# Streamed weight tiles that begin at 16 offsets, run forwards and backwards, with six raw buffers in place of seven

## The chip, the cores and the metric

One core of one Trainium2 chip runs the kernel. The metric is the device time of one execution in microseconds (us).

## The reference

One decoder layer for one sequence of 256 tokens with 4096 channels, all in float32. A conditioning vector gives shift, scale and gate; the normalised input is modulated, projected to six parts, half of the channels go through a mixture of dilated attention windows and half through causal pooling, and an output projection with a gated residual and a last normalisation follows.

```python
mod = c_act @ w_ada[l] + b_ada[l]                      # 4096 x 12288
shift, scale, gate = jnp.split(mod, 3, axis=-1)
h = rmsnorm(x, norm_gain[l])
h = h * (1.0 + scale[:, None, :]) + shift[:, None, :]
proj = jnp.einsum('bsd,dn->bsn', h, w_in[l])           # 4096 x 12288
q, k, v, g_attn, u_pool, g_pool = jnp.split(proj, ..., axis=-1)
y_attn = longnet_mixture(q, k, v).reshape(B, S, D_ATTN) * jax.nn.silu(g_attn)
y_pool = multiscale_pool(u_pool, w_pool[l], pool_scale[l]) * jax.nn.silu(g_pool)
y = jnp.concatenate([y_attn, y_pool], axis=-1) @ w_out[l]   # 4096 x 4096
x = x + gate[:, None, :] * y
return rmsnorm(x, final_gain)
```

## The kernel before

All weights are read once from HBM in float32, about 490 MB. A matrix product keeps float32 accuracy by three products of rounded operands: `w = wh + wl` and `h = hh + hl`, each part rounded to the type float32r, and `wh*hh + wh*hl + wl*hh` is summed in PSUM.

The unit of work is a *piece*: two blocks of 128 input channels by 512 output columns, one *raw* tile of 128 x 1024 float32 (512 KB). `split_piece` (L228) takes a raw tile from a ring of `RAWB` = 7, has SyncE load it (L231), ScalarE round it into `wh` (L237), and VectorE subtract for the remainder `wl` (L238). `wh` and `wl` have three buffers each, and begin on a multiple of 512 bytes (`LINE`). `products` (L241) then streams the piece through TensorE: 12 matmuls of 128 x 128 by 512 columns (L248), 8 with `wh` and 4 with `wl` as the moving operand, and `hh` or `hl` as the stationary one. The output projection uses the same function with `yh` and `yl` for `hh` and `hl`; those lie in the slots called `sa`. Of the last chunk of the output projection, the last six pieces (`HELD`) are split into such slots as well, and their second token tile goes through `prods_of_tile` (L614).

The input projection has 24 column chunks of 32 blocks; `visit` runs over them while units of two `h` blocks become ready. Raw tiles of the conditioning matrix `w_ada` run in the same ring: each is loaded by SyncE (L195, later L558) and multiplied into an accumulator, `aacc` or `gacc`, by two VectorE instructions (L161). `build_h` makes `hf`, `hh` and `hl` of a unit (L221 to L224). The gate is spread over the partitions by a float32 matmul on L565, whose moving operand is `gacc`.

A scheduler of the Tile layer sets the order on each engine; rates such as `GATE2` say how many `w_ada` tiles go with a piece. All loads are issued by SyncE in order. A raw load waits for the last reader of the tile that it overwrites. In the output projection each chunk also loads `x` (L638) and a slice of `final_gain` into the single buffer `fg` (L640), which the chunk before reads last on L672.

Of the kernel before, what the change touches and what calls it, by code (L numbers as in the profile page):

```python
# [8 lines left out]
F32R = mybir.dt.float32r  # L9
# [4 lines left out]
P = 128  # L14
# [4 lines left out]
CH = 512  # L19
# [22 lines left out]
PIECE = 2  # L42
HELD = 6
SPARE = 0
RAWB = 7
WHB = 3
WLB = 3
PSB = 2
PSMB = 4
LINE = 512  # L50
RAW = PIECE * CH
# [4 lines left out]
def tile_hybrid_block(  # L56
# [17 lines left out]
    nc = tc.nc  # L74
# [4 lines left out]
    strm = ctx.enter_context(tc.tile_pool(name="strm", bufs=2))  # L79

    def slot_a(shape, dtype=F32):
        return accp.tile(shape, dtype, name="sa", bufs=16, align_bytes=LINE)
# [7 lines left out]
    def misc():  # L90
        return ps_m.tile([P, CH], F32, name="psm")

    def raw_tile():
        return strm.tile([P, RAW], F32, name="raw", bufs=RAWB)

# [31 lines left out]
    pt = misc()  # L127
# [75 lines left out]
    def build_h(u, acc, pool, xT):  # L203
# [10 lines left out]
        for a in range(0, uk, 2):  # L214
# [10 lines left out]
            for i in range(2):  # L225
                hs[kk + i] = (hh[:, i], hl[:, i])

    def split_piece(src, n, spare=False):  # L228
        rt = raw_tile()
        v = rt.rearrange("p (k n) -> p k n", n=CH)  # L230
        nc.sync.dma_start(out=v[:, 0:n], in_=src)  # L231
        if spare:
            wh, wl = [slot_a([P, PIECE, CH], F32R) for _ in range(2)]
        else:
            wh = strm.tile([P, PIECE, CH], F32R, name="wh", bufs=WHB, align_bytes=LINE)
            wl = strm.tile([P, PIECE, CH], F32R, name="wl", bufs=WLB, align_bytes=LINE)
        nc.scalar.copy(out=wh[:, 0:n], in_=v[:, 0:n])  # L237
        nc.vector.tensor_tensor(out=wl[:, 0:n], in0=v[:, 0:n], in1=wh[:, 0:n].bitcast(F32), op=ALU.subtract)  # L238
        return wh, wl

    def products(pt, hv, wh, wl, first, last):  # L241
        n = len(hv)
        seq = [(t, i, p, wh) for i in range(n) for t in range(NT) for p in range(2)]
        seq += [(t, i, 0, wl) for t in range(NT) for i in range(n)]
        for e, (t, i, p, w) in enumerate(seq):
            started = first and not any(q[0] == t for q in seq[:e])
            ended = last and not any(q[0] == t for q in seq[e + 1:])
            nc.tensor.matmul(pt[t], lhsT=hv[i][p][:, t * P:(t + 1) * P], rhs=w[:, i], start=started, stop=ended)  # L248

    chains = []  # L250
    pending = []
# [24 lines left out]
    def visit(ch, ka, kb):  # L276
        pt = ps.tile([P, NT, CH], F32, name="mm")
        npc = -(-(kb - ka) // PIECE)
        szs = [(kb - ka) // npc + (1 if i < (kb - ka) % npc else 0) for i in range(npc)]
        k = ka  # L280
        for n in szs:
            wh, wl = split_piece(wi_v[:, k:k + n, ch * CH:(ch + 1) * CH], n)
            hv = [hs[k + i] for i in range(n)]
            products([pt[:, t] for t in range(NT)], hv, wh, wl, k == ka, k + n == kb)
            k += n
            tick(n)
        if ka == 0:
            accs[ch] = (slot_b if 8 <= ch < 16 else slot_a)([P, NT, CH])
            nc.scalar.copy(out=accs[ch], in_=pt)  # L289
        else:  # L290
            nc.vector.tensor_tensor(out=accs[ch], in0=pt, in1=accs[ch], op=ALU.add)  # L291
# [186 lines left out]
    def pool_mix(g):  # L478
# [31 lines left out]
        def lin():  # L510
            yh[4 + g] = slot_a([P, HG, S], F32R)
            yl[4 + g] = slot_a([P, HG, S], F32R)
            po = [misc(), misc()]
            wv = w_pool[0, g].rearrange("(k p) n -> p k n", p=P)
            w = [split_piece(wv[:, 2 * a:2 * a + 2], 2) for a in range(2)]
            for d in range(4):
                o = po[d // 2][:, (d % 2) * S:(d % 2 + 1) * S]
                ds = slice(d * P, (d + 1) * P)
                for c_ in range(4):
                    wh, wl = w[c_ // 2][0][:, c_ % 2, ds], w[c_ // 2][1][:, c_ % 2, ds]  # L520
                    ph, pl = k["ph"][:, c_], k["pl"][:, c_]
                    nc.tensor.matmul(o, lhsT=wh, rhs=ph, start=(c_ == 0), stop=False)  # L522
                    nc.tensor.matmul(o, lhsT=wh, rhs=pl, start=False, stop=False)  # L523
                    nc.tensor.matmul(o, lhsT=wl, rhs=ph, start=False, stop=(c_ == 3))  # L524
            for d in range(4):
                y = late.tile([P, S], F32, name="y", bufs=2)
                nc.vector.scalar_tensor_tensor(out=y, in0=po[d // 2][:, (d % 2) * S:(d % 2 + 1) * S],
                                               scalar=psc[:, g * 4 + d:g * 4 + d + 1],
                                               in1=k["sg"][:, d], op0=ALU.mult, op1=ALU.mult)
                nc.scalar.copy(out=yh[4 + g][:, d], in_=y)  # L530
                nc.vector.tensor_tensor(out=yl[4 + g][:, d], in0=y, in1=yh[4 + g][:, d].bitcast(F32), op=ALU.subtract)
                ydone[4 + g] += 1
# [51 lines left out]
    for c, ch in enumerate(order):  # L584
# [5 lines left out]
        elif 12 <= ch < 16:  # L590
            i = ch - 12
# [38 lines left out]
    def out_chunk(n):  # L630
# [12 lines left out]
        while k < KT:  # L643
            m = min(PIECE, KT - k)
            if k + 2 * PIECE >= KT > k + PIECE:
                need_gate(n)
            wh, wl = split_piece(wo_v[:, k:k + m, cs], m, n == 7 and KT - HELD * PIECE <= k < KT - SPARE * PIECE)
            while not all(ydone[kk // HG] == HG for kk in range(k, k + m)):
                tick(0)
            yv = [(yh[kk // 4][:, kk % 4], yl[kk // 4][:, kk % 4]) for kk in range(k, k + m)]  # L650
            if n == 7 and k + m > KT - HELD * PIECE:
                held.append((yv, wh, wl))
                prods_of_tile(pt, 0, held[-1:], k + m == KT)
            else:
                products(pt, yv, wh, wl, k == 0, k + m == KT)
            k += m
            tick(m)
# [79 lines left out]
```

## Time and profile before

| | |
|---|---|
| runs | 1567.26 and 1571.35 us, median 1569.3 us |
| the profiled execution's own time | 1567.34 us |
| its span, first to last instruction | 1565.4 us |
| busy: TensorE, VectorE, ScalarE | 97%, 90%, 45% |
| DMA moved | 491.11 MB, 314 GB/s on average |
| mean granted TensorE clock | 0.997 |

Times in the profile are microseconds from the start of the span, unless ns is written. PE is TensorE, PEld its weight loads, DVE is VectorE, ACT ScalarE, SP SyncE (SPq its queue, which issues the loads). A matmul's recorded duration overlaps the next one's, so its pace is read from one start to the next.

### The profile page before, as it was taken

How to read it: one execution, taken by the hardware profiler on the slowest of the kernel's cores; microseconds unless marked ns; L12 is line 12 of the kernel's file. 1: busy time of each engine (PE TensorE's matmuls, PEld its weight loads, DVE VectorE, ACT ScalarE, POOL GpSimd, SP SyncE). 2: the span in 40 equal slices, each digit the busy share in tenths (PEclk: the TensorE clock that was granted, in tenths of full speed). 3: DMA queues.
4: the chain of work that ended last, by engine and by line, in shares of the span. 5: the costliest groups of instructions: out<-in, count | busy, mean ns of one | idle time of the engine just before them, and what ended most of it. 6: DMA issues, size and time to landing. Idle time of an engine off the chain costs nothing.

```text
span 1565.4 us, 20360 instructions
## 1 busy us (share of the span) xinstructions
PE 1516.3 (97%) x7043; PEld 1257.5 (80%) x7043; DVE 1405.4 (90%) x1759; ACT 697.6 (45%) x820; POOL 0.7 (0%) x5
## 2 busy tenths in 40 slices
PE   2999999999999999999999999999999999999997
PEld 2877888888888888888888888888898888888775
DVE  5988999999999998899999998989988788898886
ACT  4655344443443434344344344556554443444433
POOL 0000000000000000000000000000000000000000
PEclk9999999999999999999999999999999999999999
DMA  9999999999999999899999998867778899998886
GB/s 331 363 335 362 321 331 321 324 308 336 327 310 327 312 330 313 294 326 326 354 340 331 330 333 307 290 226 242 231 250 273 287 357 347 318 339 324 320 305 250
DMA packets 324087, 491.11 MB, mean 314 GB/s; under 512 B 19320, under 2 KB 150664, under 8 KB 323984
## 3 DMA queue, kind: packets, MB, share of 16 engines
q1 hardware_dynamic: 323984, 489.82, 92.2%
q8 instruction: 55, 0.90, 0.2%
q14 instruction: 48, 0.39, 0.1%
HBM read 485.55 MB, written 4.19 MB: 313 GB/s over the span
## 4 chain that ended last, share of the span: by engine, by line
PE 91%; DVE 3%; DMA 3%; issue 1%; ACT 1%; SPq 0%; DVEq 0%; ACTq 0%
PE mm L248 83%; DVE aacc L161 1%; PE psm L614 1%; PE psm L248 1%; DMA raw<-in_w_ada_dram 1%; DMA raw<-in_w_in_dram 1%; PE psm L208 1%; DVE wl L238 1%; ACT wh L237 1%; PE psm L523 0%; PE psm L524 0%; PE psm L522 0%; DMA sb<-in_x_dram 0%; DMA raw<-in_w_out_dram 0%; PE psm L565 0%
## 5 line engine op out<-in xcount | busy, mean ns | idle before, releaser
L237 ACT CAST wh<-raw 128x1024 fp32r<-128x1024 f32 x514 | 538.5, 1050 | 700.0 <-PE mm L248 497.9
L238 DVE TENSOR_TENSOR wl<-raw,wh 128x1024 fp32r<-128x1024 f32 x514 | 624.5, 1218 | 45.1 <-ACT wh L237 41.9
L248 PE MATMUL mm<-wh,hh 128*128 128x512 f32 x1536 | 605.4, 394 | 4.8 <-ACT wh L237 3.8
L248 PE MATMUL mm<-wh,hl 128*128 128x512 f32 x1536 | 599.6, 390 | 0.0
L248 PE MATMUL mm<-wl,hh 128*128 128x512 f32 x1536 | 414.2, 391 | 0.6 <-DVE wl L238 0.6
L161 DVE SCALAR_TENSOR_TENSOR aacc<-raw,cact,aacc 128x512 f32<-128x512 f32 x496 | 371.0, 748 | 31.4 <-DMA raw<-in_w_ada_dram 23.8
L248 PEld LDWEIGHTS mm<-wh,hh 128*128 128x128 f32 x1536 | 288.8, 188 | 67.0 <-ACT wh L237 7.2
L248 PEld LDWEIGHTS mm<-wl,hh 128*128 128x128 f32 x1536 | 288.4, 188 | 61.1 <-DVE wl L238 1.4
L248 PEld LDWEIGHTS mm<-wh,hl 128*128 128x128 f32 x1536 | 288.9, 188 | 58.3 <-issue 0.2
L248 PE MATMUL mm<-wh,sa 128*128 128x512 f32 x896 | 224.0, 392 | 1.9 <-ACT wh L237 1.9
L248 PEld LDWEIGHTS mm<-wh,sa 128*128 128x128 f32 x896 | 167.7, 188 | 39.7 <-ACT wh L237 3.4
L161 DVE SCALAR_TENSOR_TENSOR gacc<-raw,cact,gacc 128x512 f32<-128x512 f32 x248 | 185.5, 748 | 13.5 <-DMA raw<-in_w_ada_dram 9.8
L248 PE MATMUL mm<-wl,sa 128*128 128x512 f32 x448 | 119.8, 389 | 0.0
L291 DVE TENSOR_TENSOR sa<-mm,sa 128x1024 f32<-128x1024 f32 x92 | 112.1, 1218 | 8.5 <-PE mm L248 8.4
L248 PEld LDWEIGHTS mm<-wl,sa 128*128 128x128 f32 x448 | 84.0, 188 | 17.5
L291 DVE TENSOR_TENSOR sb<-mm,sb 128x1024 f32<-128x1024 f32 x48 | 58.5, 1219 | 7.3 <-PE mm L248 7.3
L328 PE MATMUL psm<-diag_r,sb 128*128 128x128 f32 x128 | 16.9, 300 | 15.9 <-DVE diag_r L320 15.9
L221 ACT ACTIVATE hf<-xT,s 128x256 f32<-128x256 f32 x32 | 17.5, 595 | 27.9 <-DVE s L213 27.9
L328 PEld LDWEIGHTS psm<-diag_r,sb 128*128 128x128 f32 x128 | 16.6, 215 | 16.1 <-DVE diag_r L320 16.1
L289 ACT COPY sa<-mm 128x1024 f32<-128x1024 f32 x16 | 16.3, 1016 | 14.2 <-PE mm L248 14.1
L248 PE MATMUL psm<-wh,sa 128*128 128x512 f32 x80 | 20.1, 394 | 1.4 <-ACT wh L237 1.4
L248 PEld LDWEIGHTS psm<-wh,sa 128*128 128x128 f32 x80 | 14.8, 188 | 5.3 <-ACT wh L237 2.2
(113 smaller groups left out, 618.1 us busy)
## 6 DMA issues: line engine op xcount, KB each, us to landing
raw<-in_w_in_dram SPq DMA_DIRECT2D x384, 512.0 KB, 5.7
raw<-in_w_ada_dram SPq DMA_DIRECT2D x512, 256.0 KB, 5.3
raw<-in_w_ada_dram SPq DMA_DIRECT2D x128, 512.0 KB, 6.5
raw<-in_w_out_dram SPq DMA_DIRECT2D x128, 512.0 KB, 6.8
sb<-in_x_dram SPq DMA_DIRECT2D x16, 512.0 KB, 6.4
raw<-in_w_pool_dram SPq DMA_DIRECT2D x8, 512.0 KB, 4.7
out_dram<-sb SPq DMA_DIRECT2D x16, 256.0 KB, 2.6
fg<-in_final_gain_dram SPq DMA_DIRECT2D x8, 256.0 KB, 4.7
```

The lines of the kernel that those rows point to most:

```text
L161: nc.vector.scalar_tensor_tensor(out=acc, in0=r, scalar=cact[:, kt:kt + 1], in1=init if kt == 0 else acc, op0=ALU.mult, op1=ALU.add)
L208: nc.tensor.matmul(pc[:, j:j + 1], lhsT=acc[:, j * P:(j + 1) * P], rhs=ones, start=True, stop=True)
L221: nc.scalar.activation(out=hf[:, i], in_=xT[:, kk + i], func=AF.Identity, scale=s12[:, 1, a + i:a + i + 1], bias=s12[:, 0, a + i:a + i + 1])
L237: nc.scalar.copy(out=wh[:, 0:n], in_=v[:, 0:n])
L238: nc.vector.tensor_tensor(out=wl[:, 0:n], in0=v[:, 0:n], in1=wh[:, 0:n].bitcast(F32), op=ALU.subtract)
L248: nc.tensor.matmul(pt[t], lhsT=hv[i][p][:, t * P:(t + 1) * P], rhs=w[:, i], start=started, stop=ended)
L289: nc.scalar.copy(out=accs[ch], in_=pt)
L291: nc.vector.tensor_tensor(out=accs[ch], in0=pt, in1=accs[ch], op=ALU.add)
L328: nc.tensor.matmul(px[:, i * S + t * P:i * S + (t + 1) * P], lhsT=xs[q][:, t, (2 * a + i) * P:(2 * a + i + 1) * P], rhs=diag_r[:, t], star ...
L614: nc.tensor.matmul(pt[t], lhsT=h[:, t * P:(t + 1) * P], rhs=w, start=False, stop=last and e == len(seq) - 1)
```

## The change

Every tile of `wh` and `wl` grows by 128 elements (512 bytes per partition), and the piece within it begins at one of 16 offsets of 0 to 124 elements, which change after every second piece. Every second piece is marked in `back`; for these, `stream` gives the matmul its moving operand and its PSUM output with step -1, so that column 511 goes first and each result lands where it did. The ring of raw tiles has 6 tiles in place of 7. No instruction is added or taken away. In the built program 6072 matmuls pass through `stream`, 3036 of them with step -1, and 5676 begin off a multiple of 512 bytes; the weight pieces of the pooling map are used as stationary operands and begin at the offsets too, read forwards.

```diff
-RAWB = 7
+RAWB = 6
+STARTS = (0, 1, 4, 8, 16, 24, 32, 40, 48, 56, 64, 80, 96, 112, 120, 124)
...
+    count = [0]
+    back = {}
+
+    def stream(out, w, i):
+        if w.offset is not None and back.get((w.tensor.name, w.offset)):
+            return out[:, ::-1], w[:, i, ::-1]
+        return out, w[:, i]
+
     def split_piece(src, n, spare=False):
...
-            wh = strm.tile([P, PIECE, CH], F32R, name="wh", bufs=WHB, align_bytes=LINE)
-            wl = strm.tile([P, PIECE, CH], F32R, name="wl", bufs=WLB, align_bytes=LINE)
+            o = STARTS[count[0] // 2 % len(STARTS)]
+            wh, wl = [strm.tile([P, RAW + P], F32R, name=m, bufs=b, align_bytes=LINE)[:, o:o + RAW].rearrange(
+                "p (k n) -> p k n", n=CH) for m, b in (("wh", WHB), ("wl", WLB))]
+            back[wh.tensor.name, wh.offset] = back[wl.tensor.name, wl.offset] = count[0] % 2 == 1
+            count[0] += 1
...
-            nc.tensor.matmul(pt[t], lhsT=hv[i][p][:, t * P:(t + 1) * P], rhs=w[:, i], start=started, stop=ended)
+            o, m = stream(pt[t], w, i)
+            nc.tensor.matmul(o, lhsT=hv[i][p][:, t * P:(t + 1) * P], rhs=m, start=started, stop=ended)
```

The scheduler answers the smaller ring with a few other places. On ScalarE in the input projection, where a unit of `h` is built (`hf` is the modulated input, `hh` its rounding), the order before is:

```order
L237 CAST wh<-raw 128x1024 x23
L221 ACTIVATE hf<-xT,s_4390 128x256 x2
L237 CAST wh<-raw 128x1024
L223 CAST hh<-hf 128x512
L237 CAST wh<-raw 128x1024 x23
L221 ACTIVATE hf<-xT,s_4919 128x256 x2
L223 CAST hh<-hf 128x512
```

and in the changed kernel, at the same place:

```order
L249 CAST wh<-raw 128x1024 x24
L222 ACTIVATE hf<-xT,s_4390 128x256 x2
L224 CAST hh<-hf 128x512
L249 CAST wh<-raw 128x1024 x23
L222 ACTIVATE hf<-xT,s_4919 128x256 x2
L224 CAST hh<-hf 128x512
```

The rounding of the first unit's `hh` stands ahead of one weight's rounding and no longer behind it. On SyncE in the output projection, at the end of a chunk (`raw` tiles of `w_out` and `w_ada`, and `fg`, which waits for L672 of the chunk before), the order before is:

```order
L558 DMA raw_11815<-in_w_ada_dram 128x2x512 [waits DMAHW3_49,DVE_49]
L231 DMA raw_11819<-in_w_out_dram 128x2x512 [waits DMAHW4_49,DVE_49]
L558 DMA raw_11837<-in_w_ada_dram 128x2x512 [waits DMAHW5_49,DVE_49]
L231 DMA raw_11841<-in_w_out_dram 128x2x512 [waits DMAHW6_49,DVE_49]
L640 DMA fg_11733<-in_final_gain_dram 128x512 [waits DVE_49]
L558 DMA raw_11859<-in_w_ada_dram 128x2x512 [waits DMAHW7_49,DMAHW0_49,Activation_49]
```

and in the changed kernel:

```order
L571 DMA raw_11815<-in_w_ada_dram 128x2x512 [waits DMAHW4_49,DVE_49]
L240 DMA raw_11819<-in_w_out_dram 128x2x512 [waits DMAHW5_49,DVE_49]
L571 DMA raw_11837<-in_w_ada_dram 128x2x512 [waits DMAHW6_49,DVE_49]
L653 DMA fg_11733<-in_final_gain_dram 128x512 [waits DVE_49]
L240 DMA raw_11841<-in_w_out_dram 128x2x512 [waits DMAHW0_49,Activation_49]
L571 DMA raw_11859<-in_w_ada_dram 128x2x512 [waits DMAHW7_49,DMAHW1_49,DVE_49]
```

The load of `fg` stands one raw load (raw_11841) earlier.

## Rows read from the trace of the kernel before

**Rows 1.** The page: busy time by engine, and the chain that ended last.

```profile
PE 1516.3 (97%) x7043; PEld 1257.5 (80%) x7043; DVE 1405.4 (90%) x1759; ACT 697.6 (45%) x820; POOL 0.7 (0%) x5
...
PE 91%; DVE 3%; DMA 3%; issue 1%; ACT 1%; SPq 0%; DVEq 0%; ACTq 0%
PE mm L248 83%; DVE aacc L161 1%; PE psm L614 1%; PE psm L248 1%; DMA raw<-in_w_ada_dram 1%; DMA raw<-in_w_in_dram 1%; PE psm L208 1%; DVE wl L238 1%; ACT wh L237 1%; PE psm L523 0%; PE psm L524 0%; PE psm L522 0%; DMA sb<-in_x_dram 0%; DMA raw<-in_w_out_dram 0%; PE psm L565 0%
```

**Rows 2.** Windows by stage: stretch, length, busy by engine, then clock, DMA share, GB/s.

```profile
60.00:300.00 240.00, 235.53 (x1037) 192.20 (x1036) 222.84 (x260) 114.43 (x118) 0.00 (x0) 0.99 0.99 334
300.00:900.00 600.00, 599.04 (x2682) 497.21 (x2681) 564.59 (x647) 241.35 (x244) 0.00 (x0) 1.00 0.97 325
900.00:1250.00 350.00, 349.41 (x1821) 294.14 (x1821) 312.65 (x491) 180.20 (x245) 0.53 (x1) 1.00 0.82 271
1250.00:1500.00 250.00, 248.06 (x1085) 203.15 (x1084) 219.20 (x241) 102.65 (x114) 0.00 (x0) 1.00 0.93 335
```

**Rows 3.** Timeline of TensorE over one piece: start, duration, what [idle before].

```profile
700.46 0.39 PE L248 MATMUL mm<-wh,hh 128*128 128x512 f32 x1
...
702.28 1.07 PE L248 MATMUL mm<-wl,hh 128*128 128x512 f32 x4
703.18 0.39 PE L248 MATMUL mm<-wh,hh 128*128 128x512 f32 x1
```

**Rows 4.** The same after a wait of TensorE near 80 us.

```profile
79.58 0.50 PE L248 MATMUL mm<-wh,hh 128*128 128x512 f32 x1 [2.05 <-ACT wh L237]
79.92 0.39 PE L248 MATMUL mm<-wh,hl 128*128 128x512 f32 x1
...
80.62 0.48 PE L248 MATMUL mm<-wh,hh 128*128 128x512 f32 x1
...
81.32 0.63 PE L248 MATMUL mm<-wh,hh 128*128 128x512 f32 x1
81.75 0.63 PE L248 MATMUL mm<-wh,hl 128*128 128x512 f32 x1
82.17 1.91 PE L248 MATMUL mm<-wl,hh 128*128 128x512 f32 x4
```

**Rows 5.** The same around the gate's broadcast at 1361 us.

```profile
1361.06 1.02 PE L565 MATMUL psm<-gacc,ones_m 128*128 128x512 f32 x2
1361.52 1.72 PE L248 MATMUL mm<-wh,sa 128*128 128x512 f32 x5
```

**Rows 6.** Waits of SyncE's queue: us in total, times, longest.

```profile
SPq L231 <- DVE wl L238: 324.2, 280, 5.4
...
SPq L640 <- DVE sb L672: 42.1, 7, 9.5
```

**Rows 7.** Waits of the engines, same columns.

```profile
ACT wh L237 <- PE mm L248: 497.9, 314, 4.3
ACT wh L237 <- DMA raw<-in_w_out_dram: 82.1, 49, 5.7
ACT wh L237 <- DMA raw<-in_w_in_dram: 81.3, 46, 3.9
...
PE mm L248 <- ACT wh L237: 5.8, 5, 2.0
```

**Rows 8.** The page's groups: count, busy us, mean ns, idle before and its releaser.

```profile
L237 ACT CAST wh<-raw 128x1024 fp32r<-128x1024 f32 x514 | 538.5, 1050 | 700.0 <-PE mm L248 497.9
L238 DVE TENSOR_TENSOR wl<-raw,wh 128x1024 fp32r<-128x1024 f32 x514 | 624.5, 1218 | 45.1 <-ACT wh L237 41.9
```

**Rows 9.** Loads of 300:900, 1250:1500 and 1020:1110 us: median us to landing.

```profile
raw<-in_w_in_dram SPq DMA_DIRECT2D x217, 512.0 KB, 5.6
...
raw<-in_w_out_dram SPq DMA_DIRECT2D x90, 512.0 KB, 7.0
...
DMA packets 11128, 21.53 MB, mean 239 GB/s; under 512 B 653, under 2 KB 653, under 8 KB 11122
...
raw<-in_w_in_dram SPq DMA_DIRECT2D x21, 512.0 KB, 4.7
```

**Rows 10.** Timeline of SyncE's queue at a chunk end.

```profile
1415.09 0.37 SPq L558 DMA_DIRECT2D raw<-in_w_ada_dram  x1
1423.23 0.35 SPq L640 DMA_DIRECT2D fg<-in_final_gain_dram  x1
```

**Rows 11.** Timeline at the next chunk end.

```profile
1472.94 1.04 ACT L237 CAST wh<-raw 128x1024 fp32r<-128x1024 f32 x1 [5.71 <-DVE gacc L161]
...
1474.03 2.11 PE L248 MATMUL mm<-wh,sa 128*128 128x512 f32 x8 [1.94 <-ACT wh L237]
```

## The prediction

> **What bounds the kernel now.** I read the busy shares and the chain first, then windows by stage, then single matmuls, then the rows of the ring of raw buffers. TensorE is busy 97% of the span, and 91% of the chain that ended last is its own work, 83% on the line of the streamed products; DMA holds 3% of the chain and VectorE 3% [rows 1]. So the price of one streamed matmul sets the time. From 700.46 to 703.18 us the twelve matmuls of one piece follow each other: 2.72 us, 226.7 ns each, while the clock is granted in full (1.00 in all middle windows, [rows 2, 3]). There are 512 streamed pieces (24 chunks of the input projection and 8 of the output projection, 16 each), 6144 matmuls: 6144 x 226.7 ns = 1393 us of the 1565.4. The rest is the start, attention and pooling on the same engine, waits and the end.
>
> DMA is close behind: its engines are 97 to 99% busy in the projections until 900 us, 82% in the next stage, 93% in the output projection [rows 2]. What hides it is the ring of raw tiles. SyncE nearly always finds the ring full and waits for a last reader, 280 times for the remainder on L238 alone [rows 6], while ScalarE waits 314 times for TensorE to give back a rounded tile and only 95 times for a weight to land [rows 7]; TensorE itself waits for a rounded tile in the products only 5 times, 5.8 us [rows 7].
>
> The profiled execution took 1567.3 us, its span and 1.9 us around it; the median of the runs is 2.0 us above it. Sums are made against 1567.3 and carried over to the median.
>
> **Part 1: the starts.** No instruction is added. In the built program 6072 of the 6144 streamed matmuls go through the new helper (72 of the last chunk read held tiles as before), and 5676 of them now begin off a 512-byte line, most of them by a multiple of 32 bytes. What that costs TensorE no row shows, since every streamed operand begins on a line. Three bounds. The nearest row is the gate's broadcast on L565, whose moving operand lies 288 bytes past a line (by the built program's addresses): its two records take 0.46 us, 230 ns for 512 columns, though in full fp32 [rows 5]. The dearest rows of aligned products at the full clock are those just after a wait: from 79.92 to 80.62 us three matmuls take 0.70 us, 233 ns each [rows 4]. So a price is 0 to 6.5 ns per matmul: 0 to 5676 x 6.5 = 37 us. Below nothing: the pace holds about 13 ns that don't scale with the clock. Between 81.32 and 82.17 us, right after a wait of 2.05 us, two matmuls take 0.85 us, 425 ns for the 512 columns [rows 4]; so the clock was at the lower of its two levels (1.2 and 2.4 GHz), and half of it is 213 ns, 13.5 less than 226.7. Were they a quarrel over where the two operands lie, up to 5676 x 13.5 = 77 us could go. I take 0: the pace is the same for the wh and the wl products, for both halves of a tile and beside any VectorE or ScalarE work in the stretch shown [rows 3], so no sign of a quarrel over addresses is in the trace. ScalarE's and VectorE's writes to the new starts are taken at nothing too: their 1050 and 1218 ns [rows 8] read a raw tile that lies 352 bytes past a line already, ScalarE is idle 700 us, and a slower write hides as long as the two rounded tiles ahead do.
>
> The Trainium skill's page "TensorE: Matmul & The Clock Gate" (Wait — 56ns, not 53.3ns?) gives 512 columns / 2.4 GHz + 2.5 ns, 215.7 ns, for such a stream; the rows show 226.7, so the measurement decides, and by the page alone 11 ns of each matmul would be there to win (about 62 us).
>
> **Part 2: back to front.** 3036 matmuls read the rounded tile and write PSUM with step -1. No row has a negative step on any engine. Nothing if the operand is fetched and written in the same groups either way. At the other end one column every second clock: that is the price at the clock's lower level, 0.43 us from 81.32 to 81.75 in place of 0.227 [rows 4], so 3036 x 0.2 = 607 us. I choose 0, as the same words are touched in the same lines, but keep the other end as a rival.
>
> **Part 3: six raw tiles.** A tile is 512 KB. In 300 to 900 us it comes every 524,288 B / 325 GB/s = 1.61 us, so with seven a tile lives 11.3 us: 5.6 to land [rows 9], 1.05 + 1.22 in its two readers [rows 8], 3.4 to spare. With six it is 9.7 us, 1.8 to spare: nothing lost. In the output projection (335 GB/s, 1.57 us) seven give 11.0: 7.0 to land, 2.3 read, 1.7 spare; six give 9.4 and 0.1 spare. That still carries the rate, since a landing shortens when fewer are under way (4.7 us at 239 GB/s [rows 9]), but there is no reserve. It is needed at the chunk ends, where the load of final_gain waits on SyncE for L672 with all later raw loads behind it: no issue between 1415.09 and 1423.23 us, and 42.1 us in 7 waits in all [rows 6, 10]. Mostly the ring covers that; at 1474.03 us it does not, and TensorE waits 1.94 us [rows 11]. One tile less is 1.57 us less cover: 0 to 7 x 1.57 = 11 us. I take 1.6 for the end that fails already and 0.7 for the other six: 6 us. Among the five early waits of TensorE (5.8 us, [rows 7]) I charge two with one tile: 3 us; there DMA is at its limit (99%) and the number of tiles matters less. A longer wait can cost clock as well: after the one of 2.05 us at 79.58, six matmuls ran at the lower level, some 1.2 us [rows 4]; two or three such are in the range.
>
> **Part 4: what moves.** The order shows hh's rounding ahead of a weight's cast and not behind it, on an engine with 700 us idle: 0. The load of final_gain stands one raw load earlier, which is the same lost tile.
>
> Sum: 0 + 0 + 6 + 3 = +9 us: 1576 for the profiled one, **1578 us** at the median. With the ring's ends 0 and +22 (11 at the chunk ends, 8 for all five early waits, 3 of clock) this case runs from 1566 to 1593.
>
> **Rivals.** (a) *A start off the line costs a little.* Every product off a line takes 230 to 233 ns: 19 to 37 us and the ring's 9, 1597 to 1615. For it: the two rows above. Against: one is fp32, the other aligned. It passes 2% from 4 ns per matmul (5676 x 4 = 23 us beside the 9). (b) *Back to front at half pace*, slower far over 2%: 1578 + 607 = 2185. The place is TensorE's stream of every second piece; it passes 2% from 7 ns per reversed matmul (3036 x 7 = 21 us beside the 9). For it: no row of a reversed stream exists, and the start of the stream is the only thing that the change does to TensorE's inner loop. The Trainium skill's page "PSUM — Partial Sum Buffer" (Specifications) speaks for it: it says that any output that is not contiguous slows matmuls; whether a step of -1 counts, no run here shows. (c) *The fixed 13.5 ns shrink.* 77 us less on TensorE, but DMA is busy 99, 97, 82 and 93% of the four windows [rows 2], which lets through 2 us of 240, 18 of 600, all of some 20 in 350, and 17 of 250, together 57: about 1521. Against: the pace knows no other value in the undisturbed stretches.
> That the change doesn't do what it says is excluded: the built program holds the starts and the steps.
>
> **Chances.** Forecast 0.61, (a) 0.19, (b) 0.15, (c) 0.05. The range goes from 1564, the forecast without any cost of the ring and a little scatter, to 1630, (a) at its dear end with the ring at its own (1569 + 37 + 22 = 1628); (b) and (c), 0.20, are left out. About 2%, 31 us, is what a measurement can tell from no change. Faster is (c), 0.05. Slower is (b) and most of (a): 0.30. Same is the forecast and the rest of (a): 0.65.
>
> **What would show it.** Right: the twelve matmuls of a piece in 2.72 us at every offset and in both directions; waits of TensorE for ScalarE's rounding around the chunk ends, some 1 to 3 us each; landings in the output projection near 6 us; fewer waits of ScalarE for TensorE and more for DMA. Wrong: two paces that alternate piece by piece (direction) or a cycle of 32 pieces (offset); or DMA's share falling below 0.9 in 300 to 900 us with TensorE waiting there, which would mean that the spare 1.8 us was not there.

## The result and the profile after

The changed kernel takes 1607.8 us (median; 1605.1 to 1610.6), before 1569.3 us: a ratio of 1.0247, 95% interval 1.0206 to 1.0288. It is slower by 38.5 us, beyond the 2% that counts as no change.

The page of the changed kernel, in the lines that answer to [rows 1]:

```profile
PE 1550.7 (97%) x7043; PEld 1257.4 (78%) x7043; DVE 1410.7 (88%) x1759; ACT 696.9 (43%) x820; POOL 0.7 (0%) x5
...
PE 89%; DMA 4%; DVE 3%; issue 2%; ACT 1%; SPq 1%; DVEq 0%; ACTq 0%
```

TensorE is as full as before, so the span of 1603.3 us (37.9 more) is not made of waits. The windows by stage, columns as in [rows 2]:

```profile
60.00:300.00 240.00, 234.87 (x1016) 187.03 (x1015) 219.66 (x255) 113.29 (x116) 0.00 (x0) 1.00 0.98 328
300.00:900.00 600.00, 598.06 (x2601) 483.00 (x2600) 552.05 (x627) 234.75 (x238) 0.00 (x0) 1.00 0.95 314
900.00:1250.00 350.00, 349.36 (x1804) 290.45 (x1803) 310.14 (x493) 175.74 (x238) 0.53 (x1) 1.00 0.82 270
1250.00:1500.00 250.00, 248.87 (x1062) 199.13 (x1061) 210.79 (x230) 98.31 (x110) 0.00 (x0) 1.00 0.92 323
```

Between 300 and 900 us 2601 matmuls fit where 2682 did, at the same full clock; DMA serves 314 GB/s where it served 325, and its engines are less busy, not more. The timeline of TensorE, as in [rows 3], shows where each matmul got dearer. The program's order tells which piece is which: at 327.19 us a piece at offset 0 forwards, at 329.94 one at offset 0 back to front, at 332.74 one at offset 1 forwards, at 335.59 the same back to front; at 364.44 one at offset 32 back to front.

```profile
327.19 0.39 PE L261 MATMUL mm<-wh,hh 128*128 128x512 f32 x1
...
329.03 1.07 PE L261 MATMUL mm<-wl,hh 128*128 128x512 f32 x4
329.94 0.40 PE L261 MATMUL mm<-wh,hh 128*128 128x512 f32 x1
...
331.81 1.10 PE L261 MATMUL mm<-wl,hh 128*128 128x512 f32 x4
332.74 0.40 PE L261 MATMUL mm<-wh,hh 128*128 128x512 f32 x1
...
335.59 0.40 PE L261 MATMUL mm<-wh,hh 128*128 128x512 f32 x1
...
364.44 0.40 PE L261 MATMUL mm<-wh,hh 128*128 128x512 f32 x1
...
367.32 0.39 PE L261 MATMUL mm<-wh,hh 128*128 128x512 f32 x1
```

From piece to piece: 2.75 us, 2.80, 2.85, and 2.88 us for the last; before, the piece of [rows 3] took 2.72. Over all undisturbed starts of the trace (from one start to the next under 250 ns) a streamed matmul takes 227.0 ns before and 233.2 after: 6144 x 6.2 = 38 us, as much as the span has grown. By direction it is 232.3 ns forwards and 234.1 back to front. Waits of the engines, as in [rows 7], tell that the ring has become tighter without TensorE noticing much:

```profile
ACT wh L249 <- PE mm L261: 462.9, 277, 7.6
ACT wh L249 <- DMA raw<-in_w_in_dram: 128.2, 76, 4.6
ACT wh L249 <- DMA raw<-in_w_out_dram: 114.0, 64, 5.9
```

ScalarE waits for a landing 140 times where it waited 95 times. ScalarE's rounding and VectorE's remainder cost what they cost, 1048 and 1220 ns (1050 and 1218 in [rows 8]), so writing at the new starts is free for them. The waits of SyncE's queue, as in [rows 6]:

```profile
SPq L240 <- DVE wl L250: 332.2, 237, 6.6
...
SPq L653 <- DVE sb L685: 18.9, 7, 4.2
```

The waits for `fg` at the chunk ends fell from 42.1 us to 18.9. That is no gain: the raw load ahead of `fg` now waits in its place. SyncE's queue at the chunk end that answers to [rows 10]:

```profile
1446.59 0.37 SPq L571 DMA_DIRECT2D raw<-in_w_ada_dram  x1
1452.68 0.37 SPq L240 DMA_DIRECT2D raw<-in_w_out_dram  x1
```

The load of `fg` follows at 1457.22 us. Over the seven chunk ends, the gap in the queue before `fg` and the one before the load ahead of it come to 51.8 us together in the kernel before and to 46.8 here.

### The profile page after: what moved, and what is told of

It is laid out like the page before. It is cut to its first block, busy times and chain, and to the rows that moved or that the text cites. A ratio compares the mean times of both kernels' runs of the same rounds, so it can differ in the third digit from the quotient of the medians.

```text
span 1603.3 us, 20336 instructions
## 1 busy us (share of the span) xinstructions
PE 1550.7 (97%) x7043; PEld 1257.4 (78%) x7043; DVE 1410.7 (88%) x1759; ACT 696.9 (43%) x820; POOL 0.7 (0%) x5
## 4 chain that ended last, share of the span: by engine, by line
PE 89%; DMA 4%; DVE 3%; issue 2%; ACT 1%; SPq 1%; DVEq 0%; ACTq 0%
PE mm L261 81%; DMA raw<-in_w_ada_dram 2%; DVE aacc L162 2%; DVE wl L250 1%; PE psm L627 1%; PE psm L261 1%; DMA raw<-in_w_out_dram 1%; DMA raw<-in_w_in_dram 1%; PE psm L209 1%; ACT wh L249 1%; DMA sb<-in_x_dram 0%; PE psm L537 0%; PE psm L535 0%; PE psm L536 0%; PE psm L424 0%
## 5 line engine op out<-in xcount | busy, mean ns | idle before, releaser
L249 ACT CAST wh<-raw 128x1024 fp32r<-128x1024 f32 x514 | 537.5, 1048 | 739.4 <-PE mm L261 462.9
L250 DVE TENSOR_TENSOR wl<-raw,wh 128x1024 fp32r<-128x1024 f32 x514 | 624.8, 1220 | 48.5 <-ACT wh L249 43.2
L261 PE MATMUL mm<-wh,hh 128*128 128x512 f32 x1536 | 614.0, 400 | 6.5 <-ACT wh L249 4.8
L261 PE MATMUL mm<-wh,hl 128*128 128x512 f32 x1536 | 609.1, 397 | 0.0
L261 PE MATMUL mm<-wl,hh 128*128 128x512 f32 x1536 | 423.5, 397 | 0.6 <-DVE wl L250 0.6
L261 PE MATMUL mm<-wh,sa 128*128 128x512 f32 x896 | 229.7, 399 | 3.1 <-ACT wh L249 3.1
L678 DVE TENSOR_TENSOR yo<-mm,gt 128x1024 f32<-128x1024 f32 x7 | 8.6, 1224 | 13.2 <-PE mm L261 13.2
```

What stands on the lines that cost most here:

```text
L261: nc.tensor.matmul(o, lhsT=hv[i][p][:, t * P:(t + 1) * P], rhs=m, start=started, stop=ended)
L678: nc.vector.tensor_tensor(out=y[:, tp], in0=src, in1=gt.unsqueeze(1).to_broadcast(w), op=ALU.mult)
```

## The experiments

All have six raw tiles and the padded rounded tiles of the changed kernel. The theory was that each streamed matmul got dearer by the place and direction of its operand; the rivals were the ring of six, and that only the *change* from one piece to the next costs. The pace is the mean from one start to the next over the undisturbed starts. The first four ran on one chip with the kernel before (1568.2 us there).

**e1_ring6: the ring alone.**

```diff
-STARTS = (0, 1, 4, 8, 16, 24, 32, 40, 48, 56, 64, 80, 96, 112, 120, 124)
+STARTS = (0,)
...
-            back[wh.tensor.name, wh.offset] = back[wl.tensor.name, wl.offset] = count[0] % 2 == 1
+            back[wh.tensor.name, wh.offset] = back[wl.tensor.name, wl.offset] = False
```

> The changed kernel with all tiles begun at offset 0 and read forwards: what is left of the change is the ring of six raw tiles (and the padding of the rounded tiles). Address theory (each streamed matmul costs more off a line or back to front, and that is all of the loss): a piece in 2.72 us, ratio 1.000 to 1.003. Rival, the ring as the prediction priced it: +9 us, ratio 1.006. Rival, the ring as the main cause: ratio 1.02.

Measured: 1579.4 us, ratio 1.0068 (1.0051 to 1.0085), by that ratio +10.7 us. The pace is 227.1 ns. So dearer matmuls alone would not be the whole story: the ring by itself costs about what the prediction charged for it, but not where. Waits of the engines and of SyncE's queue, and a part of TensorE's timeline, all of this run:

```profile
ACT wh L249 <- DMA raw<-in_w_in_dram: 197.6, 116, 4.7
ACT wh L249 <- DMA raw<-in_w_out_dram: 116.2, 63, 7.5
...
PE mm L261 <- ACT wh L249: 9.7, 8, 2.0
```

```profile
SPq L653 <- DVE sb L685: 18.9, 7, 4.2
```

```profile
594.67 0.77 PE L261 MATMUL mm<-wh,hh 128*128 128x512 f32 x1 [1.67 <-DVE sa L304]
...
627.26 0.96 PE L261 MATMUL mm<-wl,hh 128*128 128x512 f32 x3 [1.42 <-DVE wl L250]
...
651.52 0.47 PE L261 MATMUL mm<-wh,hh 128*128 128x512 f32 x1 [0.83 <-DVE sb L304]
...
675.72 0.47 PE L261 MATMUL mm<-wh,hh 128*128 128x512 f32 x1 [0.80 <-ACT wh L249]
...
1484.86 1.48 PE L261 MATMUL mm<-wh,sa 128*128 128x512 f32 x3 [2.02 <-ACT wh L249]
```

Counted from streamed matmul 2000 to 3000 (516 to 756 us), the run loses 7.3 us more than before, and 3.4 us more from 5500 to 6000 near the end; each of the other stretches of 500 differs by under 1 us. The larger part lies in the input projection, where the prediction had found 1.8 us to spare per tile and charged only the early waits. There, from 516 to 756 us, ScalarE waits 54 times for a `w_in` tile to land, 99.3 us in all, where before it waited 15 times, 29.3 us. VectorE, for which TensorE waits at 594.67, had itself waited 3.06 us for a `w_ada` tile. Some of the loss is clock: after the waits at 594.67 and 1484.86 five and eight matmuls run at 0.43 us each, the lower of its two levels (granted 0.50 from 595.2 to 597.4 us and 0.54 from 1484.8 to 1488.3), together some 3 us.

**e2_offsets: the 16 offsets, all forwards** (`back` set to False as in e1, `STARTS` left).

> The 16 offsets alone, every piece read forwards, six raw tiles. Address theory: in the trace of the changed kernel forward pieces go at 232.2 ns per matmul over all offsets, so 6144 x (232.2 - 227.0) = +32 us, about 1601. If the step -1 is what costs, and the offsets only look dear because every piece follows a reversed one: 1570 to 1575.

Measured: 1604.8 us, ratio 1.0236 (1.0215 to 1.0256); the pace is 232.2 ns. The offsets alone cost 5.1 ns per matmul, and 25 us beside e1.

**e3_alternate: every second piece back to front, all at offset 0** (`STARTS = (0,)`).

> Every second piece back to front, all at offset 0, six raw tiles. Address theory: back to front at offset 0 goes at 233.6 ns, forward pieces between them at 228.7, so 6144 x (231.1 - 227.0) = +25 us, about 1594. If the offsets are what costs: 1570 to 1575.

Measured: 1595.5 us, ratio 1.0172 (1.0153 to 1.0191); pace 233.6 ns back to front and 228.4 forwards.

**e4_all_back: every piece back to front, at offset 0** (`STARTS = (0,)`, `back` set to True).

> Every piece back to front, all at offset 0, six raw tiles. If the step itself costs: 233.6 ns per matmul, +40 us, about 1609, more than when every second piece is reversed. Rival, only the change from one piece to the next costs, as after a wait: 227 ns again, 1570.

Measured: 1610.8 us, ratio 1.0275 (1.0257 to 1.0292); 233.4 ns for every matmul. The direction itself costs 6.3 ns. So the rival that only the change of direction costs falls; only some 1.3 ns on the forward pieces of e3 come from it.

The others ran once each, with the kernel before at 1565.1 to 1570.7 us beside them. They are read against e1, and above all by their pace, a mean over more than 5700 starts.

**e9_read_back and e10_write_back: which side of the reversal costs.** Both from e4, with the helper's return cut in two:

```diff
-            return out[:, ::-1], w[:, i, ::-1]
+            return out, w[:, i, ::-1]        # e9
+            return out[:, ::-1], w[:, i]     # e10
```

> Every piece is read back to front at offset 0, but its PSUM output is written forwards, so each 512-column chunk comes out mirrored and the layer's output is changed by that; the work is the same. If the read of the moving operand is what costs 6.3 ns: 233.3 ns per matmul, about 1610. If the write to PSUM costs: 227 ns, about 1579.

> Every piece is read forwards at offset 0, but written to PSUM back to front, so each 512-column chunk comes out mirrored; the work is the same. If the PSUM write with step -1 costs: 233.3 ns per matmul, about 1610. If the read costs: 227 ns, about 1579.

Measured: e9 1611.0 us and 233.4 ns, e10 1580.8 us and 227.1 ns. One piece of TensorE's timeline in e9 and then in e10:

```profile
700.29 0.40 PE L261 MATMUL mm<-wh,hh 128*128 128x512 f32 x1
...
702.16 1.10 PE L261 MATMUL mm<-wl,hh 128*128 128x512 f32 x4
703.09 0.40 PE L261 MATMUL mm<-wh,hh 128*128 128x512 f32 x1
```

```profile
700.91 0.39 PE L261 MATMUL mm<-wh,hh 128*128 128x512 f32 x1
...
702.73 1.07 PE L261 MATMUL mm<-wl,hh 128*128 128x512 f32 x4
703.63 0.39 PE L261 MATMUL mm<-wh,hh 128*128 128x512 f32 x1
```

2.80 us against 2.72 for the piece: the read from SBUF with step -1 is the whole price, and the write to PSUM with step -1 is free.

**e5_start64, e6_start32, e7_start1: one offset throughout, forwards** (`STARTS = (64,)`, `(32,)`, `(1,)`).

> Every piece begins 64 elements (256 bytes) past a 512-byte line, forwards, six raw tiles. In the traces with 16 offsets this one reads like offset 0. If the cost goes by the address modulo 256 bytes: 227 ns per matmul, time as with the ring alone, about 1579. If a whole 512-byte line counts: 230 ns or more, 1595 and up.

> Every piece begins 32 elements (128 bytes) past a line, forwards, six raw tiles; the offset never changes. If the address itself costs: 233 ns per matmul as in the runs with changing offsets, about 1605. Rival, only a change of address from piece to piece costs: 227 ns, about 1579.

> Every piece begins 1 element (4 bytes) past a line, forwards, six raw tiles; stationary tiles on the line. Address theory: 236.8 ns per matmul as with changing offsets, 60 us over the ring alone, about 1639. If the change from piece to piece were part of that price: less, down to 233 ns, about 1616.

Measured: 1582.5 us at 227.1 ns; 1608.5 us at 232.5 ns; 1632.5 us at 237.8 ns. The address costs also when it never changes, and 256 bytes further on costs nothing. The time of e7 is 6 us under the one expected although its pace is above it: the starts that are 250 ns or more apart cost 24.2 us above the pace in e7 and 33.3 in e1, so at the slower pace the ring gives most of its own cost back.

**e8_both32 and e11_stat32: whose address it is.** The stationary tiles of the input projection are moved as well, with `STARTS = (32,)` in e8 and `(0,)` in e11; both give up one buffer of the attention scratch (`sm`, not shown):

```diff
-                htile[kk // HB] = [pool.tile([P, HB, S], F32R, name=n, align_bytes=LINE) for n in ("hh", "hl")]
+                ht = pool.tile([P, 2 * HB * S + P], F32R, name="hh", align_bytes=LINE)
+                htile[kk // HB] = [ht[:, 32 + j * HB * S:32 + (j + 1) * HB * S].rearrange("p (k s) -> p k s", s=S) for j in range(2)]
```

> Moving tiles and, in the input projection, the stationary ones (hh and hl, now halves of one tile) both begin 128 bytes past a line; the output projection's stationary tiles stay on the line. One buffer of the attention scratch is given up for the room. If the distance between the two operands is what counts: 227 ns in the input projection and 232.4 in the output projection. If each operand's own address counts: 232 ns or more in both.

> Only the stationary tiles of the input projection begin 128 bytes past a line; the moving ones stay on it. If the distance counts: some 232 ns in the input projection, 227 in the output projection. If only the moving operand's own address counts: 227 ns in both, time as with the ring alone, about 1579.

Measured: e8 1592.4 us, 227.2 ns in the input projection and 232.4 in the output projection; e11 1603.3 us, 232.5 and 227.1 ns. From TensorE's timeline of e8, a piece of the input and one of the output projection:

```profile
700.42 1.98 PE L262 MATMUL mm<-wh,hh 128*128 128x512 f32 x8
702.23 1.07 PE L262 MATMUL mm<-wl,hh 128*128 128x512 f32 x4
703.14 1.52 PE L262 MATMUL mm<-wh,hh 128*128 128x512 f32 x6
...
1352.05 2.02 PE L262 MATMUL mm<-wh,sa 128*128 128x512 f32 x8
1353.90 1.09 PE L262 MATMUL mm<-wl,sa 128*128 128x512 f32 x4
1354.83 1.56 PE L262 MATMUL mm<-wh,sa 128*128 128x512 f32 x6
```

and the same two of e11:

```profile
699.90 2.03 PE L262 MATMUL mm<-wh,hh 128*128 128x512 f32 x8
701.76 1.10 PE L262 MATMUL mm<-wl,hh 128*128 128x512 f32 x4
702.70 2.03 PE L262 MATMUL mm<-wh,hh 128*128 128x512 f32 x8
...
1350.50 1.98 PE L262 MATMUL mm<-wh,sa 128*128 128x512 f32 x8
1352.31 1.07 PE L262 MATMUL mm<-wl,sa 128*128 128x512 f32 x4
1353.22 1.98 PE L262 MATMUL mm<-wh,sa 128*128 128x512 f32 x8
```

In e8 the piece whose operands are both 128 bytes past a line takes 2.72 us, the one where only the moving operand is takes 2.78; in e11, 2.80 where only the stationary operand is and 2.72 where neither is. The distance between the two operands is what counts, taken within a line of 512 bytes: how far each begins past a multiple of 512 bytes, one less the other.

**e12_other_starts: is there a better distance?** (`STARTS = (2, 3, 5, 6, 10, 12, 14, 18, 20, 28, 36, 44, 52, 60, 62, 63)`, all forwards.)

> Sixteen other offsets between 2 and 63 elements in turn, all forwards, six raw tiles, stationary tiles on the line: is there a distance at which a matmul takes less than the 226.7 ns of distance 0? If distance 0 is the best one there is: every offset between 227 and 240 ns, time 1600 to 1630. If the fixed 13 ns are themselves a quarrel over addresses: some offset near 215 ns, which would make a kernel that beats both.

Measured: 1605.9 us, 232.6 ns. Matched to the program's order, the mean start-to-start in ns by offset in elements, forwards (undisturbed gaps; e2, then e12):

```
0:228.0 1:236.8 4:231.8 8:233.3 16:229.0 24:233.7 32:233.2 40:234.0 48:233.3 56:233.1 64:227.8 80:229.7 96:232.6 112:233.5 120:233.1 124:232.6
2:233.6 3:229.5 5:239.5 6:234.2 10:233.9 12:232.7 14:232.5 18:233.8 20:231.2 28:227.4 36:233.1 44:233.0 52:233.9 60:231.3 62:232.7 63:229.5
```

No offset beats 227, so no version faster than the kernel before was in sight.

## Why the prediction came out as it did

The range held the time because rival (a), at a chance of 0.19, lay inside it; the likeliest case, no change at 1578 us, did not happen. 1607.8 us is rival (a), with a small price of the direction beside it. By the runs, the ring costs 11 us (e1), the offsets 25 more (e2 against e1) and the direction 3 more (the changed kernel against e2). Both signs that the prediction named as wrong are in the trace: a pace that goes by offset and one that goes by direction.

**Part 1 failed at "I take 0".** The offsets cost 5.1 ns per matmul in the mean (e2), near the dear end of the bounds 0 to 6.5, and 9.7 ns there at offset 1 and 12.4 at offset 5 of e12, outside them. The reason given for 0 was that the pace is even, so that no quarrel over addresses shows. But before, every streamed moving and stationary operand began on a 512-byte line; a trace in which the distance never varies can't show what the distance costs. The row that did vary, L565 with an operand off its line, lay 3.3 ns above and was set aside because of its type. The Trainium skill would have spoken for 0 as well: "TensorE: Matmul & The Clock Gate" (Step-by-step: what each phase is for) says that the weight load and the moving operand have read ports of their own, so that the next load takes nothing from the running matmul. e8 and e11 differ from that: the same matmul takes 227.2 or 232.5 ns by the distance of the two operands alone. The bound below nothing was misread too: halving 425 ns halves a fixed part with it, so by these two rows such a part would be 2 x 226.7 - 425 = 28 ns and not 13.5. No run won any of it (e12).

**Part 2 was mis-sized.** It chose 0 of 0 to 200 ns per reversed matmul; e4 gives 6.3 ns where the offset is 0. Beside offsets that are dear already the step adds less: in the changed kernel 1.8 ns in the mean (234.1 against 232.3), 3036 x 1.8 = 5 us, and 3.0 us by the times of the changed kernel and e2. The price of one column every second clock in rival (b) has no support. The reason "the same words are touched in the same lines" fails for the read (e9) and holds for the write (e10). The rule of the Trainium skill's page "PSUM — Partial Sum Buffer" (Specifications) that an output which isn't contiguous slows matmuls doesn't reach a step of -1: 227.1 ns in e10.

**Part 3 had the sum right, in part by luck.** +9 was charged, e1 measures +10.7. In the steady flow it had found 1.8 us to spare per tile, an average, and charged nothing; 7.3 us were lost there, between 516 and 756 us. That an uneven arrival of the tiles is what such an average hides fits ScalarE's longer waits for landings, and no run isolates it. The early waits, charged with 3 us, cost 0.8 (the first 500 streamed matmuls). At the chunk ends 6 us were charged and 3.4 lost near the end, at the place it named: TensorE waited for a rounded tile once before, 1.94 us [rows 11], and twice in e1, 1.52 us at 1441.43 and 2.02 at 1484.86. e5 and e10, with the same ring and pace as e1, lose at the same three places: 7.6 and 8.8 us, 2.6 and 2.8, 3.5 and 1.5. The bounds of this case come out as 1569 to 1591 by its own sum; 1566 to 1593 allows for a scatter that the sum doesn't name.

**The parts don't add.** The pace's 38 us and the ring's 10.7 would make 49; measured are 38.5. With dearer matmuls TensorE asks for 314 GB/s and not 325, and the ring of six carries that better: what the starts of streamed matmuls that are 250 ns or more apart cost above the pace comes to 33.3 us in e1, 24.6 in the changed kernel and 23.2 before. How much is given back varies: with a pace of 232 to 233 ns it is 28.4 in e2 and 32.9 in e6. The prediction added the ring's 9 us to rival (a) as if the two were apart.

**Part 4 and rival (c).** Nothing in the runs is put down to the moved rounding of ScalarE, as part 4 had it, but no run tests it alone. Rival (c) falls: no offset or direction made a matmul cheaper (e12).

## What to carry to other kernels

Where TensorE streams float32r tiles without a break, moving and stationary tiles that begin equally far past a 512-byte line keep the best pace seen here. At most other distances a matmul of 227 ns costs 2 to 12 ns more, in the dearest run 4% of the kernel with the ring's part in it (e7, 1632.5 us against 1567.7). An even row says nothing about a quantity that is the same in all of it: bound its price by the row where it differs, even if that row differs in more. And costs on two resources that hide each other need not add: a slower TensorE forgives some of a smaller ring.

## What the runs showed of the hardware

The pace of a float32r matmul of 512 columns depends on the distance in SBUF between its moving operand and the stationary operands, taken within a line of 512 bytes: 227.1 ns at distance 0 and at 256 bytes (e1, e5), 232.5 at 128 bytes whichever of the two is moved (e6, e11), 227.2 when both are (e8), 237.8 at 4 bytes (e7). It does not run evenly with the distance: 227.4 ns at 112 bytes but 233.7 at 96, 239.5 at 20 (e12, e2). A read with step -1 costs 6.3 ns at offset 0, and in the changed kernel no offset brings it under 233.2; at offset 32 it takes 239.0 where the forward read takes 232.2. A PSUM write with step -1 costs nothing (e10, 227.1 ns). What inside the read makes this is open. A ring of seven with the new starts was not tried, since the padded tiles leave no room for it.
